# Hybrid diffusion block on one core: expert weights applied at the slots, and another order for layer 0's first rows

## The chip, the core and the metric

One core of a Trainium2 chip runs the whole kernel in one launch. Its engines are TensorE (PE, matmuls; PEld its weight loads), VectorE (DVE), ScalarE (ACT), GpSimd (POOL) and SyncE (SP, which here only issues DMAs); ACT and POOL also issue DMAs on queues of their own. The 16 DMA engines of the core move all data between HBM and the on-chip memories, SBUF and PSUM. The metric is the device time of one execution in microseconds, lower is better.

## What is computed

Two layers over 512 latent tokens and 256 context tokens of width 1024. Each layer is a mixer and then a mixture of experts; the last layer computes no context output. Cut to what matters here:

```python
for l in range(2):
    sh1, sc1, gt1, sh2, sc2, gt2 = split6(silu(c) @ w_ada[l] + b_ada[l])       # the same for the context, from c_ctx
    lam = exp(sum(lq1 * lk1)) - exp(sum(lq2 * lk2)) + lam_init
    xn = rms_norm(h, g_norm_mix[l]) * (1 + sc1) + sh1
    p = xn @ w_in[l]                       # then attention, gating MLP, neighbourhood attention
    h = h + gt1 * merge_branches(...)
    xn2 = rms_norm(h, g_norm_ffn[l]) * (1 + sc2) + sh2
    h = h + gt2 * hier_moe(xn2)            # top-1 group, top-2 experts, weights top_w
    ...
return rms_norm(h, g_final)
def hier_moe(x):                           # each token: two experts, expert e with weight top_w
    ys = (silu(xb @ w_gate[e]) * (xb @ w_up[e])) @ w_down[e]
    return segment_sum(ys[dest] * w_sorted[:, None], ...)
```

So a token's residual gets gt2 * (w0 * y0 + w1 * y1), y0 and y1 from its two experts.

## The kernel before, in words

All values are float32. A product of the mixer is made of three matmuls on a high and a low part of each factor (`wh`, `wl` of the weights, made by `wsplit`; `xh`, `xl` of the rows, made by `modulate`, or by `high` and `low`), so that each weight unit of 256 columns costs 24 matmuls of 128x256 per row tile of 128 tokens. There are six row tiles, four latent (0 to 3) and two of the context (4 and 5). SP issues all weight loads from one program order; where a buffer is still in use, the issue waits.

**Start of layer 0** (`mixer`, lines 460 to 481 and the constants from line 170). SP issues the small loads (`cvec`, `vecs`, `bada`, `gsub`, `lamv`, `rbias`), then six row tiles of `x`, the first `w_in` unit and the eight halves of `w_ada`. For each row tile `rownorm` squares the rows on ACT (line 220), makes the factor on DVE and POOL (221, 222; POOL's pow takes the root) and scales the rows in place on ACT (224). PE transposes the scaled rows, four row tiles for each k of eight (`turn`, 400). `ada` multiplies the conditioning vector with `w_ada` in 32 small matmuls for each half (445), DVE adds the halves (448, 451), PE transposes the sum (453) and DVE writes it to `mod` (454); `scales` makes the factors of the modulation (392, 394). `modulate` then applies scale and shift on ACT while reading PSUM (407) and splits on DVE (408, 409). All this is done for four k, then for the other four. Then the products of the first unit run over the six row tiles (230 to 232), the context's turns and modulations between them, each followed by a gelu on ACT (490).

**Expert stream** (`moe`). The router has sorted the tokens to 17 lanes of 128 slots (the two weights of each token are in `topw`). For each lane, POOL gathers the rows of `xs` by index (`gather`, line 1909), PE transposes them (1923), `gateup` and `down` multiply with the experts' weights, which SP streams in 1 MB pieces in lane order (1933), ACT and DVE copy the two halves of the result from PSUM (1972, 1973), and POOL scatters the lane's 128 rows to the table `yb`, one row for each token and choice (1974). Stages of neighbouring lanes overlap: the down product of a lane runs behind the gate and up products of the next. A loop at the end handles blocks over the fixed lanes; its length is read from memory (2020). Near the end of the stream SP loads the gate rows `grow` (gt2, broadcast to all partitions).

**Combine** (class `Combine`). For a row tile SP loads both rows of each token from `yb` (2053). `pre` multiplies the second by its weight on ACT (2058), `add` multiplies the first and adds on DVE (2064) and multiplies by the gate row (2066), `resid` adds to the residual on DVE or POOL (2069), then come the square on ACT (2073), the root (221, 222), and either `diag` (a diagonal of the factors, 2080, which PE uses as the moving matrix to transpose and scale at once, 502) or, at the very end, `final` (2087) and a store. Between the layers, `first_units` runs this with the first two units of layer 1's mixer. Its order is set by a planner, `Weave`: each step has a list of engine times, and the planner places steps on engines, with `way` as the choice between two engines (DVE or POOL, ACT or DVE).

## Time and profile before

| | us |
|---|---|
| median of the runs shown (3 runs, 2616.36 to 2624.96) | 2620.15 |
| the profiled execution's own time | 2619.65 |
| its span in the trace | 2617.5 |
| PE busy | 2307.9 |
| DVE busy | 1123.2 |
| ACT busy | 690.7 |
| POOL busy | 384.6 |

The span is the time from the first to the last event in the trace; the execution's own time has 2.15 us around it. In order of time the program is: mixer 0 to about 895 us, expert stream 0 to about 1400, the combine with the first units of layer 1 to 1467, the rest of mixer 1 to about 2075, expert stream 1 to about 2577, and the last combine. A row of a timeline gives the start, the duration, the engine (SPq is SP's queue), the line of the kernel, the operation, the result and its operands, the number of instructions merged in it, and in brackets the idle time before with what ended it. In a row of windows the engines stand in the order PE, PEld, DVE, ACT, POOL. A PE row's "x16" is one stretch of 16 matmuls. The clock column gives the granted clock of PE as a share of its full 2.4 GHz.

### The profile page before, as it was taken

How to read it: one execution, taken by the hardware profiler on the slowest of the kernel's cores; microseconds unless marked ns; L12 is line 12 of the kernel's file. 1: busy time of each engine (PE TensorE's matmuls, PEld its weight loads, DVE VectorE, ACT ScalarE, POOL GpSimd, SP SyncE). 2: the span in 40 equal slices, each digit the busy share in tenths (PEclk: the TensorE clock that was granted, in tenths of full speed). 3: DMA queues.
4: the chain of work that ended last, by engine and by line, in shares of the span. 5: the costliest groups of instructions: out<-in, count | busy, mean ns of one | idle time of the engine just before them, and what ended most of it. 6: DMA issues, size and time to landing. Idle time of an engine off the chain costs nothing. (4 is left out here: it accounts for less than half of the span.)

```text
span 2617.5 us, 35788 instructions
## 1 busy us (share of the span) xinstructions
PE 2307.9 (88%) x14117; PEld 1563.5 (60%) x14117; DVE 1123.2 (43%) x2122; ACT 690.7 (26%) x1345; POOL 384.6 (15%) x335
## 2 busy tenths in 40 slices
PE   5999999899999799898885999999999799887983
PEld 4888788788887633333323788887777633332321
DVE  3456667677754611111004646676454611110103
ACT  4235656612212100000003325655222200000001
POOL 0101210222211101000000302212332000000002
PEclk8999999999999899999998999999999899999997
DMA  6311121265435599999997411123653799999994
GB/s 242 124 67 37 57 73 50 101 219 183 162 113 229 207 402 424 424 424 423 422 424 284 161 65 52 39 85 109 233 201 138 307 391 420 420 419 416 416 413 189
DMA packets 116714, 625.98 MB, mean 239 GB/s; under 512 B 17440, under 2 KB 23328, under 8 KB 57536
## 3 DMA queue, kind: packets, MB, share of 16 engines
q1 hardware_dynamic: 93232, 576.61, 55.8%
q0 software_dynamic: 13088, 32.60, 3.5%
q10 hardware_dynamic: 10224, 14.46, 1.5%
q8 instruction: 113, 1.85, 0.3%
q14 instruction: 57, 0.47, 0.1%
HBM read 599.93 MB, written 38.34 MB: 244 GB/s over the span
## 5 line engine op out<-in xcount | busy, mean ns | idle before, releaser
L1933 PE MATMUL pd<-ew,mh 128*32 128x512 f32 (+2 forms) x1472 | 259.6, 595 | 16.3 <-DMA ew<-in_w_down 12.2
L230 PE MATMUL pg<-xh,wh 128*128 128x512 f32 (+1 forms) x576 | 205.7, 357 | 0.0
L232 PE MATMUL pg<-xh,wl 128*128 128x512 f32 (+1 forms) x576 | 205.4, 357 | 0.0
L709 PE MATMUL pj<-xh,wh 128*128 128x512 f32 (+1 forms) x544 | 195.9, 360 | 10.8 <-DVE rt L829 3.9
L231 PE MATMUL pg<-xl,wh 128*128 128x512 f32 (+1 forms) x576 | 205.3, 356 | 0.0
L711 PE MATMUL pj<-xh,wl 128*128 128x512 f32 (+1 forms) x544 | 189.4, 348 | 0.0
L710 PE MATMUL pj<-xl,wh 128*128 128x512 f32 (+1 forms) x544 | 189.3, 348 | 0.0
L1933 PEld LDWEIGHTS pd<-ew,mh 128*32 128x32 f32 (+2 forms) x1472 | 90.6, 122 | 159.3 <-issue 116.2
L1933 PE MATMUL pu<-ew,mx 128*32 128x512 f32 (+2 forms) x768 | 154.4, 609 | 29.4 <-DMA ew<-in_w_up 29.3
L364 DVE SCALAR_TENSOR_TENSOR jk<-wr,crow 128x1024 bf16<-128x1024 f32 x128 | 155.7, 1217 | 47.6 <-DMA wr<-in_w_adaT 45.2
L1933 PE MATMUL pg<-ew,mx 128*32 128x512 f32 (+2 forms) x768 | 152.7, 609 | 21.2 <-DMA ew<-in_w_gate 21.1
L1951 DVE TENSOR_TENSOR mh<-mh,pu 128x512 f32<-128x512 f32 x34 | 23.4, 688 | 331.0 <-PE pu L1933 331.0
L1974 POOL DMA_INDIRECT yb<-mt,si x34 | 37.1, 1093 | 850.2 <-DVE mt L1973 577.9
L213 POOL TENSOR_TENSOR wl<-wr,wh 128x1024 fp32r<-128x1024 f32 x48 | 119.6, 2491 | 282.2 <-ACT wh L212 282.2
L1933 PE MATMUL pg<-ew,mt 128*32 128x512 f32 (+2 forms) x704 | 140.3, 623 | 17.9 <-DMA ew<-in_w_gate 16.9
L1933 PE MATMUL pu<-ew,mt 128*32 128x512 f32 (+2 forms) x704 | 134.4, 596 | 20.9 <-DMA ew<-in_w_up 20.7
L1973 DVE COPY mt<-pd 128x512 f32<-128x512 f32 x34 | 23.5, 692 | 282.9 <-ACT mt L1972 274.3
L1950 ACT ACTIVATE mh<-pg 128x512 f32<-128x512 f32 x34 | 20.3, 597 | 459.0 <-PE pg L1933 459.0
L1322 ACT ACTIVATE sg<-pg 128x512 f32<-128x512 f32 x72 | 38.0, 528 | 369.7 <-PE pg L232 362.1
L938 PE MATMUL S<-K,Q 128*128 128x256 f32 (+3 forms) x544 | 111.8, 333 | 12.9 <-ACT E L976 6.2
L1960 DVE COPY mh<-trh 128x512 f32<-128x512 f32 x34 | 23.5, 691 | 226.0 <-PE trh L1957 226.0
L709 PEld LDWEIGHTS pj<-xh,wh 128*128 128x128 f32 x544 | 102.8, 189 | 29.5 <-DVE rt L829 5.5
(369 smaller groups left out, 4801.8 us busy)
## 6 DMA issues: line engine op xcount, KB each, us to landing
ew<-in_w_gate SPq DMA_DIRECT2D x128, 1024.0 KB
ew<-in_w_up SPq DMA_DIRECT2D x128, 1024.0 KB
ew<-in_w_down SPq DMA_DIRECT2D x128, 1024.0 KB
wr<-in_w_in SPq DMA_DIRECT2D x54, 1024.0 KB
wr<-in_w_adaT SPq DMA_DIRECT2D x80, 512.0 KB
br<-in_w_branch SPq DMA_DIRECT2D x24, 512.0 KB
adw<-in_w_ada SPq DMA_DIRECT2D x8, 1024.0 KB
wr<-in_w_out SPq DMA_DIRECT2D x8, 1024.0 KB
```

The costliest lines, as they stand in the source:

```text
L213: (eng or V).tensor_sub(lo, x, hi.bitcast(F32))
L230: PE.matmul(ps, lh, rh, start=(i == 0), stop=False)
L231: PE.matmul(ps, lh, rl, start=False, stop=False)
L232: PE.matmul(ps, ll, rh, start=False, stop=(i == n - 1))
L364: V.scalar_tensor_tensor(jk, ad["t"][:, i % 2 * D:(i % 2 + 1) * D], 1.0, ad["c"][:, s], op0=ALU.mult, op1=ALU.mult, accum_out=modT[al][:, ...
L709: PE.matmul(ps, lh, rh, start=(k == 0), stop=False)
L710: PE.matmul(ps, lh, rl, start=False, stop=False)
L711: PE.matmul(ps, ll, rh, start=False, stop=(k == KC - 1))
L938: PE.matmul(ps, q[:, m, part, c], K[:, m, ks], start=(part == 0), stop=(part == 1))
L1322: S.activation(sg[:, o:o + n], ps[:, :n], AF.Sigmoid)
L1933: PE.matmul(ps[o:o + r], lt[:, k0 + k, o:o + r], w[:, k, c], start=(k0 + k == 0), stop=(k0 + k == kk - 1), **pos)
L1974: G.indirect_dma_start(out=yb[l], out_offset=bass.IndirectOffsetOnAxis(ap=idx, axis=0), in_=y, in_offset=None, bounds_check=2 * TT - 1, oo ...
```

## The change

Four things change.

**Start of layer 0.** SP issues `x` 0 to 3 first, then the halves of `w_ada` 0 and 2, the first `w_in` unit, `w_ada` 1 and 3, `x` 4 and 5 and only then `lamv`, `gsub` and `rbias`; `vecs` and `bada` are issued by ACT. The exponential of lambda is POOL's pow, later (`lambdas`). The rows are not scaled: `scale_of` makes a diagonal of factors, and `turn` multiplies with it instead of a transpose. The sums of the modulation are apart from its products (`adasum`) and have a PSUM tile of their own; the split of the first unit lies between. The first two row tiles' products begin with the first four k (`share`) ahead of the last four modulations.

**Expert stream.** `topw` is transposed by PE, copied, and written by a POOL DMA to a table `tw` in DRAM, in the row order of `yb`. `weigh` gathers a lane's 128 weights from it by the scatter's indices into a column of `wsl`. The gate rows are loaded at the stream's start on ACT's queue; in layer 0 `gates` picks the latent or the context gate for each slot (the difference of the rows times a 0/1 mask, plus one of them). Two DVE steps multiply the down product by weight and gate as they read PSUM, instead of the two copies. The buffers of `y`, `hd` and `ht` are single instead of double.

**Combine.** `pre` and the multiply by the gate go, `add` is one addition, and `resid` is on DVE alone.

**Planner.** Costs change, and steps of the two ways that share a port are named "V+P" and "G+P".

```diff
     S.activation(cpad[:, :, 0:2], cvec, AF.Silu)
     vecs = const.tile([128, 4, KC], F32, name="vecs")
-    SP.dma_start(vecs, a["gvec"])
+    S.dma_start(vecs, a["gvec"])
     bada = const.tile([128, 2, 48], F32, name="bada")
-    SP.dma_start(bada, a["b_ada"])
+    S.dma_start(bada, a["b_ada"])
     gsub = const.tile([128, 2], F32, name="gsub")
...
+    def lambdas(pool):
+        lamv = pool.tile([128, 2, 4, 64], F32, name="lamv")
+        SP.dma_start(lamv, a["lam"].rearrange("(o l) f d -> o l f d", o=1).to_broadcast([128, 2, 4, 64]))
+        SP.dma_start(gsub, a["gsub"])
+        SP.dma_start(rbias, a["rbias"].rearrange("(o l) e -> o l e", o=1).to_broadcast([128, 2, 36]))
...
+        lx = ls.rearrange("p l i -> p (l i)")
+        V.memset(lamv[:, 0, 2, :4], math.e)
+        G.tensor_tensor(lx, lamv[:, 0, 2, :4], lx, op=ALU.pow)
...
+        def scale_of(nt):
+
+            r = rownorm(nm, xr[nt // 3][:, nt % 3, :], None)
+            dg0[nt] = nm.tile([128, 128], F32, name=f"dg{nt}")
+            V.tensor_scalar_mul(dg0[nt], ident, r)
...
-                PE.transpose(ps[:, i * 128:(i + 1) * 128], xr[nt // 3][:, nt % 3, k * 128:(k + 1) * 128], ident)
+                PE.matmul(ps[:, i * 128:(i + 1) * 128], xr[nt // 3][:, nt % 3, k * 128:(k + 1) * 128], dg0[nt],
+                          start=True, stop=True)
...
-            ps = pp.tile([128, 512], F32, tag="pj", name="adaps", bufs=2)
+            ps = part[n, half] = adb[half]
             for k in range(4):
                 for g in range(4):
                     PE.matmul(ps[32 * g:32 * g + 32, :128], cpad[:, 4 * half + k, :], w[:, k, g * 128:(g + 1) * 128],
                               start=(k == 0), stop=(k == 3), tile_position=(0, 32 * g))
+
+        def adasum(n, half):
+
+            ps = part.pop((n, half))
...
+            def xload(*tiles):
+                for nt in tiles:
+                    SP.dma_start(xr[nt // 3][:, nt % 3, :], a["x"][nt * 128:(nt + 1) * 128, :])
+
             raws = []
-            for n in (0, 2, 1, 3):
+
+            def aload(n):
                 for half in range(2):
                     t = nm.tile([128, KC, 256], F32, tag="ada", name="adw", bufs=8)
                     SP.dma_start(t, a["w_ada"][n, half])
                     raws.append((n, half, t))
-            for nt in range(6):
-                x = xr[nt // 3][:, nt % 3, :]
-                rownorm(nm, x, x)
-            wsplit(0)
+
+
+            xload(*range(4))
+            aload(0)
+            aload(2)
+            pump(1)
+            aload(1)
+            aload(3)
+            xload(4, 5)
+            lam = lambdas(nm)
+            next(lam)
+            for nt in range(4):
+                scale_of(nt)
...
+            def adas(four, split=None):
+
+                for i, x in enumerate(four):
+                    ada(*x)
+                    if i:
+                        adasum(*four[i - 1][:2])
+                    if split is not None and i in (1, 2):
+                        wsplit(0, 1)
+                adasum(*four[-1][:2])
+
+            adas(raws[:4])
+            scales(0, 4)
+            for k in range(4):
+                modulate(k, 0, ps[k])
+            ps = [turn(k, 0) for k in range(4, KC)]
+            adas(raws[4:], 0)
+            scales(4, KC)
+            early = {nt: pp.tile([128, 512], F32, tag="pj", name="pjx", bufs=2) for nt in range(2)}
+
+            def share(nt, k0, k1):
+                c = slice(nt * 128, nt * 128 + 128)
+                wh, wl = ready[0]
+                for k in range(k0, k1):
+                    PE.matmul(early[nt][:, :256], xk(xh, k, c), wh[:, k], start=(k == 0), stop=False)
+                    PE.matmul(early[nt][:, :256], xk(xh, k, c), wl[:, k], start=False, stop=False)
+                    PE.matmul(early[nt][:, :256], xk(xl, k, c), wh[:, k], start=False, stop=(k == KC - 1))
+
+            for nt in range(2):
+                share(nt, 0, 4)
+            for k in range(4, KC):
+                modulate(k, 0, ps[k - 4])
+            for nt in (4, 5):
+                scale_of(nt)
+            for nt in range(2):
+                share(nt, 4, KC)
+            cps = [turn(k, 1) for k in range(4)]
...
+                row_bc(grow["l"], rows(l, 3)[0], S)
...
+        def gates(n):
+
+            if last:
+                return grow["l"]
+            V.scalar_tensor_tensor(grow["s"], grow["d"], msl[:, n:n + 1], grow["l"], op0=ALU.mult, op1=ALU.add)
+            return grow["s"]
+
+        def weigh(n, idx):
+
+            G.indirect_dma_start(out=wsl[:, n:n + 1], out_offset=None, in_=tw[l],
+                                 in_offset=bass.IndirectOffsetOnAxis(ap=idx, axis=0),
+                                 bounds_check=2 * TT - 1, oob_is_err=False)
...
-            y = yo_[i % 2]
-            S.copy(y[:, :512], pd[:, :512])
-            V.tensor_copy(y[:, 512:], pd[:, 512:])
+            y = yo_[0]
+            for c in (slice(0, 512), slice(512, D)):
+                V.scalar_tensor_tensor(y[:, c], pd[:, c], wsl[:, n:n + 1], g[:, c], op0=ALU.mult, op1=ALU.mult)
...
+        trw = pp.tile([128, 512], F32, tag="tr", name="trw", bufs=2)
+        PE.transpose(trw[:2 * NT, :128], route.topw.rearrange("p k n -> p (k n)"), ident)
+        rws = ep.tile([12, 128], F32, name="rws")
+        V.tensor_copy(rws[:2 * NT], trw[:2 * NT, :128])
+        G.dma_start(tw[l].rearrange("(r p) o -> r (p o)", p=128), rws[:2 * NT])
+        for i in range(2):
+            weigh(plan[i], si[:, plan[i]:plan[i] + 1])
+        if not last:
+            V.tensor_copy(msl[:, :NS], gi)
+            V.tensor_scalar(msl[:, :NS], msl[:, :NS], TL - 0.5, None, op0=ALU.is_gt)
...
+                    weigh(n, si[:, n:n + 1])
+            if not i and not last:
+                row_bc(grow["d"], rows(l, 3)[1], S)
+                V.tensor_sub(grow["d"], grow["d"], grow["l"])
...
-        grow = raw_tile("ex").rearrange("p (k d) -> p k d", k=2)
-        for s in range((NT + 3) // 4):
-            row_bc(grow[:, s, :], rows(l, 3)[s])
...
-            def pre(self, nt):
+            def add(self, nt):
                 y = y2[nt]
-                self.done.add(nt)
-                S.activation(y[:, 1, :], y[:, 1, :], AF.Copy, scale=route.topw[:, 1, nt:nt + 1])
-
-            def add(self, nt):
-                if nt not in self.done:
-                    self.pre(nt)
-                y = y2[nt]
-                V.scalar_tensor_tensor(y[:, 0, :], y[:, 0, :], route.topw[:, 0, nt:nt + 1], y[:, 1, :],
-                                       op0=ALU.mult, op1=ALU.add)
-                V.tensor_mul(y[:, 0, :], y[:, 0, :], grow[:, nt // 4, :])
-
-            def resid(self, nt, way):
-                (V, G)[way].tensor_add(hrow(nt), hrow(nt), y2[nt][:, 0, :])
+                V.tensor_add(y[:, 0, :], y[:, 0, :], y[:, 1, :])
+
+            def resid(self, nt):
+                V.tensor_add(hrow(nt), hrow(nt), y2[nt][:, 0, :])
```

On SP, the start of the program: before, all small loads stand ahead of `x` (`x_159` and `x_160` are its two buffers of three row tiles, `adw` the halves of `w_ada`, `wr` a unit of `w_in`).

```order
3 L175 DMA vecs<-in_gvec 128x32
4 L177 DMA bada<-in_b_ada 128x96
5 L179 DMA gsub<-in_gsub 128x2
6 L181 DMA lamv<-in_lam 128x512
7 L183 DMA rbias<-in_rbias 128x72
8 L460 DMA x_159<-in_x 128x1024 x3
9 L460 DMA x_160<-in_x 128x1024 x3
10 L297 DMA wr<-in_w_in 128x2048
11 L466 DMA adw<-in_w_ada 128x2048 x8
```

The same place with the change (`x_142` and `x_143` are the buffers of `x`):

```order
2 L170 DMA cvec<-in_cond 128x16
3 L481 DMA x_142<-in_x 128x1024 x3
4 L481 DMA x_143<-in_x 128x1024
5 L488 DMA adw<-in_w_ada 128x2048 x4
6 L303 DMA wr<-in_w_in 128x2048
7 L488 DMA adw<-in_w_ada 128x2048 x4
8 L481 DMA x_143<-in_x 128x1024 x2
9 L188 DMA lamv<-in_lam 128x512
10 L189 DMA gsub<-in_gsub 128x2
11 L190 DMA rbias<-in_rbias 128x72
```

Four row tiles of `x` stand behind `cvec` alone now, the first unit of `w_in` in the middle of `w_ada`, and the last two row tiles and three small loads behind all of it.

On DVE, the last combine, before: a row tile has two steps ahead of its residual, three of the four residual adds are on POOL and don't stand here (`en` and `ew` hold the two rows of `yb`, `ex` the gate row or the final gain, `hr` the residual, `rn` the factors).

```order
1712 L2064 SCALAR_TENSOR_TENSOR ew<-ew,topw 128x1024
1713 L2066 TENSOR_TENSOR ew<-ew,ex 128x1024
1714 L2064 SCALAR_TENSOR_TENSOR ew<-ew,topw 128x1024
1715 L2066 TENSOR_TENSOR ew<-ew,ex 128x1024
1716 L2064 SCALAR_TENSOR_TENSOR ew<-ew,topw 128x1024
1717 L2066 TENSOR_TENSOR ew<-ew,ex 128x1024
1718 L221 TENSOR_SCALAR rn<-rn 128x1
1719 L2064 SCALAR_TENSOR_TENSOR en<-en,topw 128x1024
1720 L2066 TENSOR_TENSOR en<-en,ex 128x1024
1721 L221 TENSOR_SCALAR rn<-rn 128x1
1722 L2069 TENSOR_TENSOR hr<-hr,en 128x1024
```

The same place with the change:

```order
1755 L2162 TENSOR_TENSOR ew<-ew 128x1024
1756 L2165 TENSOR_TENSOR hr<-hr,ew 128x1024
1757 L2162 TENSOR_TENSOR ew<-ew 128x1024
1758 L227 TENSOR_SCALAR rn<-rn 128x1
1759 L2165 TENSOR_TENSOR hr<-hr,ew 128x1024
1760 L2162 TENSOR_TENSOR ew<-ew 128x1024
1761 L227 TENSOR_SCALAR rn<-rn 128x1
1762 L2165 TENSOR_TENSOR hr<-hr,ew 128x1024
1763 L2162 TENSOR_TENSOR en<-en 128x1024
1764 L227 TENSOR_SCALAR rn<-rn 128x1
1765 L2165 TENSOR_TENSOR hr<-hr,en 128x1024
```

DVE adds the two rows of a token and then adds them to the residual, tile by tile, with every residual add on DVE.

On POOL, a stretch of layer 1's expert stream, before: gathers of rows and scatters of results in turn.

```order
232 L1909 DMA mx<-xs_143,gi 128x1024
233 L1974 DMA yb_145<-mt,si 1024x1024
234 L1909 DMA mx<-xs_143,gi 128x1024
235 L1974 DMA yb_145<-mt,si 1024x1024
236 L1909 DMA mx<-xs_143,gi 128x1024
```

The same stretch with the change:

```order
263 L1982 DMA mx<-xs_126,gi 128x1024
264 L2047 DMA wsl<-tw_124,si 128x1
265 L2063 DMA yb_128<-mt,si 1024x1024
266 L1982 DMA mx<-xs_126,gi 128x1024
267 L2047 DMA wsl<-tw_124,si 128x1
268 L2063 DMA yb_128<-mt,si 1024x1024
269 L1982 DMA mx<-xs_126,gi 128x1024
```

Behind each gather of rows there is now a gather of weights for the same lane, ahead of the scatter of an earlier lane.

## Rows read from the trace of the kernel before

**Rows 1.** The page, PE's busy tenths in 40 equal slices of the span.
```profile
PE   5999999899999799898885999999999799887983
```

**Rows 2.** Windows: stretch, length, busy us (instructions) by engine, PE's clock, DMA share, GB/s.
```profile
8.00:41.50 33.50, 14.53 (x159) 11.71 (x160) 8.43 (x28) 18.11 (x25) 3.30 (x6) 0.84 1.02 425
...
100.00:700.00 600.00, 572.83 (x3836) 503.77 (x3835) 395.27 (x758) 259.91 (x569) 100.44 (x91) 1.00 0.31 104
950.00:1380.00 430.00, 382.20 (x1998) 136.88 (x1987) 53.14 (x112) 27.14 (x46) 30.28 (x28) 0.99 1.01 423
...
1420.00:1460.00 40.00, 33.27 (x228) 31.69 (x228) 31.77 (x51) 17.44 (x35) 11.42 (x9) 0.84 0.27 105
```

**Rows 3.** Timeline of SP's queue, start of the program.
```profile
3.54 3.77 SPq L460 DMA_DIRECT2D x<-in_x  x6
```

**Rows 4.** Timeline of ACT, 0 to 80 us.
```profile
9.92 1.06 ACT L220 ACTIVATE jk<-x 128x1024 f32<-128x1024 f32 x1 [1.24 <-DMA x<-in_x]
...
11.92 1.15 ACT L224 ACTIVATE x<-x,rn 128x1024 f32<-128x1024 f32 x1 [0.86 <-POOL rn L222]
...
38.02 2.79 ACT L407 ACTIVATE xn<-nt,mod,mA 128x512 f32<-128x512 f32 x4 [7.73 <-DVE mA L394]
49.43 2.79 ACT L407 ACTIVATE xn<-nt,mod,mA 128x512 f32<-128x512 f32 x4 [8.62 <-DVE mA L394]
...
55.25 0.39 ACT L490 ACTIVATE vv<-pjx 128x256 f32<-128x256 f32 x1 [1.74 <-PE pjx L232]
...
71.82 0.38 ACT L490 ACTIVATE vv<-pjx 128x256 f32<-128x256 f32 x1 [2.45 <-PE pjx L232]
74.64 0.38 ACT L490 ACTIVATE vv<-pjx 128x256 f32<-128x256 f32 x1 [2.44 <-PE pjx L232]
```

**Rows 5.** Timeline of PE, the last two halves of the modulation.
```profile
46.01 1.95 PE L445 MATMUL adaps<-adw,cpad 128*32 128x128 f32 x64
```

**Rows 6.** Timeline between the layers, all engines.
```profile
1411.84 1.28 DVE L2064 SCALAR_TENSOR_TENSOR ew<-ew,topw 128x1024 f32<-128x1024 f32 x1 [0.32 <-ACT ew L2058]
1413.16 1.23 DVE L2066 TENSOR_TENSOR ew<-ew,ex 128x1024 f32<-128x1024 f32 x1
1414.42 1.22 DVE L2069 TENSOR_TENSOR hr<-hr,ew 128x1024 f32<-128x1024 f32 x1
...
1418.85 0.29 DVE L2080 TENSOR_SCALAR ew<-ident,rn 128x128 f32<-128x128 f32 x1 [0.69 <-POOL rn L222]
...
1419.19 3.78 PE L502 MATMUL nt<-ew,hr 128*128 128x128 f32 x16 [20.30 <-DVE ew L2080]
...
1447.12 3.36 POOL L2069 TENSOR_TENSOR ex<-ex,en 128x1024 f32<-128x1024 f32 x1 [3.61 <-DVE en L2066]
...
1448.28 3.29 DVE L2066 TENSOR_TENSOR ew<-ew,ex 128x1024 f32<-128x1024 f32 x1
...
1454.44 0.58 PE L230 MATMUL pjx<-wh,xh 128*128 128x256 f32 x1 [2.74 <-DVE xh L524]
...
1467.12 0.40 PE L709 MATMUL pj<-xh,wh 128*128 128x512 f32 x1
```

**Rows 7.** Timeline of the last combine, all engines.
```profile
2587.03 1.15 ACT L2058 ACTIVATE ew<-ew,topw 128x1024 f32<-128x1024 f32 x1 [10.69 <-DMA ew<-yb]
...
2592.09 3.25 DVE L2066 TENSOR_TENSOR ew<-ew,ex 128x1024 f32<-128x1024 f32 x1
...
2609.46 1.28 DVE L2087 SCALAR_TENSOR_TENSOR en<-hr,rn,ex 128x1024 f32<-128x1024 f32 x1
```

**Rows 8.** DMA view of 0.5 to 4 us: packets by size, and the queue's share.
```profile
DMA packets 606, 0.14 MB, mean 39 GB/s; under 512 B 576, under 2 KB 576, under 8 KB 606
...
q1 hardware_dynamic: 606, 0.14, 17.6%
```

**Rows 9.** The page: the software queue (packets, MB, share), and POOL's scatters.
```profile
q0 software_dynamic: 13088, 32.60, 3.5%
...
L1974 POOL DMA_INDIRECT yb<-mt,si x34 | 37.1, 1093 | 850.2 <-DVE mt L1973 577.9
```

141 lines of the change are left out of this document (73 added, 68 removed).

## The prediction

> **What bounds the kernel now.** I read the page first for the shape: TensorE (PE) is busy for over 70% in nearly all slices, with the first, one in the middle and the last the lowest or near it [rows 1]. Then the windows by stage, which say what holds the full slices. In the first mixer PE works 572.83 of 600 us while the DMA engines are busy for 0.31: PE is the bound. In the expert stream the DMA engines are at 1.01 and PE works 382.20 of 430: the stream is the bound, at 423 GB/s [rows 2]. So what ends the lead-in of a mixer or a stream earlier moves all that follows, and what adds to a stream's transfers lengthens it. Three places are neither: the first 50 us, some 65 us between the layers, and the last 40 us. For these I read the timelines.
>
> Start. The DMA engines are busy from 8 to 41.5 us (1.02, 425 GB/s) [rows 2], yet PE's first product waits for a chain: ACT squares a row tile (1.06), waits 0.86 for the root and scales it (1.15), 3.07 us a round and six rounds, before it modulates the first four k at 38.02 and the last four at 49.43; the first product is done by 55.25 [rows 4]. x is issued only at 3.54 [rows 3].
>
> Between the layers. For one row tile DVE does 1.28 + 1.23 + 1.22 us behind ACT's copy, and PE starts at 1419.19 after 20.30 us without work. Later POOL takes one residual add (3.36 us), and DVE's multiply beside it takes 3.29 instead of 1.23; PE then waits 2.74 us for DVE's cast, and the first units end at 1467.12 [rows 6].
>
> End. The same stall: DVE's multiply takes 3.25 beside a residual add on POOL, and the last final step starts at 2609.46 [rows 7].
>
> **The change part by part.**
>
> *Start.* Removed: six scalings of 1.15 and the waits of 0.86 from ACT's chain; the small loads lamv, gsub, rbias, vecs and bada from ahead of x. Moved: x 4 and 5 behind all weights, their squares behind the modulations, the context's turns between products, the products of the first four k of two row tiles ahead of the last four modulations. Added: a 128x128 diagonal per tile on DVE (0.29, as the same step between the layers [rows 6]), hidden by the wait for weights. x is now second on SP, issued about 1.2 us in instead of 3.54, and I let its first bytes land near 2.2. From there I take the stream as saturated. Up to the last half of w_ada stand four x tiles of 512 KB, eight halves of 1 MB and one w_in unit of 1 MB, 11.5 MB; at 425 GB/s that is 27.1 us, so it ends at 29.3, and with 1.7 us from the last byte to the release at 31.0. Behind it PE has 32 small matmuls: the row has 1.95 us for 64 without a break [rows 5], so 1.0, or 1.8 if the clock is low; then the sums and the transpose, 1.5 as before (46.01 + 1.95 to 49.43). The last four modulations start at 34.3 instead of 49.43: **−15.1**. The squares (4 x 1.25 from about 5 us, a root and a diagonal) are done near 11, long before the weights, so they cost nothing; without the weights' wait they would be the chain again, near 12. Further on, the gelus of the six row tiles stood at 55.25 to 74.64, 19.4 us for five products of 2.82 (71.82 to 74.64) [rows 4], so 5.3 us of holes, in which the context's modulations lay. Half of the holes should close: **−2.4**. Together −17.5. The low end is 12: x keeps its 6.4 us between issue and first square (3.54 to 9.92), and the holes stay. The high end is 20, with all holes gone. What holds the start next is the stream of weights itself.
>
> The trace has 425 and 423 GB/s in two stages [rows 2]. The Trainium skill ("DMA: Bandwidth & Descriptors", Specifications) gives a limit of about 358 GB/s from HBM for one core; by that, an estimate, the 11.5 MB would take 32 us, and the time would come out 5 us higher, at 2590. The rows decide against it.
>
> *Between the layers.* Removed per row tile: ACT's copy (1.15) and DVE's multiply (1.23); the scalar_tensor_tensor (1.28) becomes an add (1.22, as the residual). Moved: all residual adds to DVE. The first tile's data is there near 1410.6 (1411.84 less ACT's copy). Then 1.22 + 1.22 + the square (1.25) + root, diagonal and one more tile's add between them (2.6) bring PE's first turn to 1416.9, **−2.3**. DVE has 6 x (3.73 − 2.44) = 7.7 us less to do; the 2.1 us that it lost beside POOL go, and the wait of 2.74 behind them. The floor is PE's own work: eight products of 2.82 and six turns of about 2, 35 us behind 1416.9, end at 1452 against 1467.12. I take **−15** in all, since PE then waits for nothing long; the ends are −8 (DVE's steps alone) and −17.
>
> *End.* The landings stay: the first at 2587.03, the others 2.5 us apart (1 MB at 424 GB/s). With 1.22 + 1.22 on DVE behind each, the last residual ends at 2597.1; the four finals (1.25 each) run from there to 2602.2, with the last square and root beside the first of them. Before, the last ended at 2610.74: **−8.5** (−7.5 to −9.5). The stores behind it stay.
>
> *Expert streams.* Added in each lane: a gather of 128 values of 4 bytes, issued by POOL; two DVE steps of about 0.7 us from PSUM (half of 1.28) where ACT and DVE copied; in layer 0 a DVE step of 1.28 for the gate. A scatter's issue takes POOL 1.09 us, and POOL sits 850 us idle before its 34 scatters [rows 9], so another issue finds room. DVE's steps lie beside PE's wait for weights; if that cover went, a lane would lose about 1.4 us. What is left is the stream. Packets: 606, of which 576 under 512 bytes, took 17.6% of 16 engines over 3.5 us [rows 8], 16 ns each, so 128 take 0.13 us of the stream, and 34 gathers 4.4. Upper end: the software queue's mean packet, 3.5% of 16 x 2617.5 us over 13088, is 0.112 us [rows 9], so 0.9 us a gather, 30 us. Lower end: nothing, if they fit into pauses. I take 4.4, since the rows of small packets are the nearer. The gate's rows (512 KB, 1.24 us: two in layer 0, one in layer 1) come from the stream's end, where PE's last lanes hid them, to its beginning: 3.7 at most, 0 at least; I take 1.9. Together **+6.3**, 0 to 12 by these two. The weight table's transpose and copy at a stream's start lie where PE waits for the gathers of rows: nothing; if a gather of the weights comes late, DVE holds that lane's scatter, two lanes after the issue.
>
> Sum: −17.5 − 15 − 8.5 + 6.3 = −34.7. Against the profiled execution's 2619.65 (0.5 below the median of the runs shown) that is **2585**. Its ends: 2573 (20 + 17 + 9.5, nothing added) and 2604 (12 + 8 + 7.5, 12 added).
>
> **The rivals.**
>
> *A: start and boundary hardly move.* The weights' stream and DVE's casts were the bound there already, and PE, with less to do, stays at a low granted clock; the window between the layers has 0.84 [rows 2], and at the lower of the two levels (1.2 GHz against 2.4) a product takes twice 2.82. Against it: shorter waits leave PE fewer holes. With half of the low ends (6 and 4), the end's 8.5 and +6.3 it gives 2607.
>
> *B: the 4-byte gathers cost like full packets,* 30 us instead of 4.4: 2611, so 0.3% below the time of before, about what a measurement of this kernel can just tell from no change. For it: the same software queue. Against it: [rows 8]. The Trainium skill (same page and section) puts the smallest transfer at line rate at 512 bytes, with a read-modify-write below; the 16 ns are of such packets, and no run here shows them as writes of 4 bytes.
>
> *C, slower: the gathers hold the stream.* Place: the lanes; POOL's queue holds the next gather of rows behind a scatter that waits for DVE, which waits for the weights. The other parts win 41 us, less 1.9; so from 1.15 us a gather (0.144 us a packet on its engine) the streams lose more than all else wins. At 0.2 us a packet it is 1.6 x 34 = 54 us, and 2635. For it: nothing in the trace shows a 4-byte indirect gather. Against it: the mean of far larger packets is 0.112 [rows 9], and two lanes lie between issue and use.
>
> *D: the start does not follow the weights,* for one because w_in's unit or its split is late: only its low end or less (0 to 5) arrives; 2597 to 2602, inside the range.
>
> **How the numbers follow.** The forecast 0.72, D 0.10, A 0.08, B 0.06, C 0.04. The range 2571 to 2605 holds the forecast's ends and D, and leaves out A, B, C and the forecast's tails, just under 2 in 10 with them. Faster by over 0.3% (7.9 us): the forecast, D, A and a third of B, so 0.91; the same: most of B, with a little of C, 0.05; slower 0.04.
>
> **What would show it.** Right: modulations of the first four k near 22, of the last four near 34, the first product done near 40, the DMA engines full from 3 us on; between the layers no DVE step of 128x1024 over 1.4 us, and the first units over in some 50 us from the last expert instead of 68; the last final step starting 14 us after the first landing instead of 22; each stream about 3 us longer. Wrong: DVE's steps from PSUM waiting for the gathered weights, a stream longer by over 10 us, ACT still the chain of the start, or PE still waiting for DVE's casts between the layers.

## The result, and the profile after

The changed kernel takes 2590.76 us (median of 4 runs, 2588.95 to 2592.67), the kernel before in the same comparison 2618.96 us (4 runs, 2616.36 to 2624.96). The ratio is 0.9893, with a 95% interval of 0.9878 to 0.9907: 28 us faster. The forecast was 2585 us with a range of 2571 to 2605. The profiled execution took 2588.95 us, with a span of 2587.1; before it was 2619.65 and 2617.5. One execution of a kernel below, the one without gathers, fell into a slower state (2891.59 us at a granted clock of 0.74, where the others have 0.97) and is left out.

The page gives the same shape as [rows 1], with a fuller first slice:

```profile
PE   7999999899999698888886999999999789887984
```

To see where 30.4 us of span went, I cut both traces at the same events: the sixth gelu on ACT, the router's reciprocal in each layer, the end of the last fixed lane's down product, the first product of the unit that follows the first two in mixer 1, and the last final step on DVE.

| stage, us | before | change | difference |
|---|---|---|---|
| start, to the sixth gelu | 74.6 | 60.3 | −14.3 |
| rest of mixer 0, to the router's reciprocal | 840.2 | 840.5 | +0.3 |
| expert stream 0, to the end of its last fixed down product | 484.1 | 492.1 | +8.0 |
| between the layers, to the next unit's first product | 68.2 | 53.8 | −14.4 |
| rest of mixer 1, to the router's reciprocal | 624.7 | 626.2 | +1.5 |
| expert stream 1 | 483.9 | 483.6 | −0.3 |
| last combine, to the start of the last final step | 33.8 | 25.3 | −8.5 |
| from there to the end of the span | 8.1 | 5.3 | −2.8 |

The windows by stage, columns as in [rows 2], with the stream's window moved by the 14 us that it starts earlier:

```profile
8.00:41.50 33.50, 26.15 (x358) 22.32 (x357) 15.26 (x41) 11.20 (x17) 1.29 (x3) 0.95 0.96 388
100.00:700.00 600.00, 570.67 (x3822) 501.17 (x3821) 398.43 (x765) 259.11 (x567) 108.59 (x93) 1.00 0.29 103
936.00:1366.00 430.00, 379.76 (x1958) 136.99 (x1954) 82.89 (x143) 17.73 (x30) 43.56 (x41) 0.99 1.01 419
1400.00:1440.00 40.00, 28.78 (x230) 28.38 (x231) 33.99 (x62) 19.30 (x39) 6.62 (x6) 0.83 0.60 237
```

PE works 26.15 us between 8 and 41.5 us, where it worked 14.53. The stream has the same DMA share, 1.01, at 419 GB/s where it had 423. That fall is the first thing that the prediction has no step for.

The start on ACT, against [rows 4]: no scaling between the squares, the last four modulations at 36.73 instead of 49.43, the sixth gelu at 60.34 instead of 74.64.

```profile
4.87 1.06 ACT L226 ACTIVATE jk<-x 128x1024 f32<-128x1024 f32 x1 [0.85 <-DMA x<-in_x]
...
23.18 2.78 ACT L422 ACTIVATE xn<-nt,mod,mA 128x512 f32<-128x512 f32 x4 [13.05 <-DVE mA L400]
...
36.73 2.79 ACT L422 ACTIVATE xn<-nt,mod,mA 128x512 f32<-128x512 f32 x4 [8.89 <-DVE mA L400]
...
43.09 0.38 ACT L554 ACTIVATE vv<-pjx 128x256 f32<-128x256 f32 x1
...
60.34 0.38 ACT L554 ACTIVATE vv<-pjx 128x256 f32<-128x256 f32 x1 [2.44 <-PE pjx L238]
```

PE in the same time (L414 the turns, L460 the modulation's matmuls): no row waits for a weight's DMA. The second turns start when ACT has read a PSUM buffer and take 5.47 us, the matmuls of the sums come right behind them, and each later step waits for DVE's sums. The margin is small: by the semaphores in the trace the last half of `w_ada` has landed whole at 32.78, and PE comes to its matmuls at 33.85.

```profile
11.32 4.63 PE L414 MATMUL nt<-dg,x 128*128 128x128 f32 x26 [0.63 <-DVE dg L408]
15.88 1.95 PE L460 MATMUL adp<-adw,cpad 128*32 128x128 f32 x64
...
24.01 5.47 PE L414 MATMUL nt<-dg,x 128*128 128x128 f32 x32 [1.53 <-ACT xn L422]
29.41 1.95 PE L460 MATMUL adp<-adw,cpad 128*32 128x128 f32 x64
...
33.85 1.08 PE L460 MATMUL adp<-adw,cpad 128*32 128x128 f32 x32 [0.26 <-DVE mod L473]
```

Between the layers, DVE's and PE's timelines, against [rows 6]: two steps of 1.22 for a row tile and none of 3.29; PE's first turn comes 17.8 us behind the last down product's end (1392.9) instead of 20.3, and the next unit begins 36.0 us later.

```profile
1404.89 1.22 DVE L2162 TENSOR_TENSOR ew<-ew 128x1024 f32<-128x1024 f32 x1
1406.14 1.22 DVE L2165 TENSOR_TENSOR hr<-hr,ew 128x1024 f32<-128x1024 f32 x1
```

```profile
1410.69 5.35 PE L566 MATMUL nt<-ew,hr 128*128 128x128 f32 x32 [17.75 <-DVE ew L2176]
...
1446.70 0.39 PE L778 MATMUL pj<-xh,wh 128*128 128x512 f32 x1
```

The windows from the first turn to the next unit's first product, before and then after, show where the rest of the gain lies. The same matmuls (289 and 288 records) keep PE busy for 41.20 us before and 35.48 after, at a granted clock of 0.85 and 0.96; PE's idle time falls from 6.7 to 0.5 us. So of the 11.9 us that this stretch is shorter, 5.7 are matmuls that run faster and 6.2 are closed waits.

```profile
1419.19:1467.12 47.93, 41.20 (x289) 39.62 (x289) 37.88 (x63) 22.66 (x47) 11.42 (x9) 0.85 0.26 97
```

```profile
1410.69:1446.70 36.01, 35.48 (x288) 35.08 (x289) 29.17 (x61) 19.28 (x44) 5.13 (x5) 0.96 0.40 153
```

The change has one more part, which its list above leaves out: the length of the loop of blocks is read before the last lanes and not behind them. Little can come from it here: the combine's first loads are issued 6.2 us behind the last down product instead of 6.8, and its first step starts 12.0 us behind it, where it was 11.8.

The last combine on DVE, against [rows 7]: from the first landing at 2568.05 to the last final step 13.8 us, where it was 22.4.

```profile
2568.05 1.23 DVE L2162 TENSOR_TENSOR ew<-ew 128x1024 f32<-128x1024 f32 x1 [10.07 <-DMA ew<-yb]
...
2575.68 1.23 DVE L2162 TENSOR_TENSOR en<-en 128x1024 f32<-128x1024 f32 x1
...
2576.94 1.22 DVE L2165 TENSOR_TENSOR hr<-hr,en 128x1024 f32<-128x1024 f32 x1
...
2581.84 1.28 DVE L2183 SCALAR_TENSOR_TENSOR en<-hr,rn,ex 128x1024 f32<-128x1024 f32 x1
```

Behind the last final step, POOL's closing instructions (the view of the program's last line on POOL, before and then after; duration min/median/max in ns). The longest DRAIN takes 9.49 us before and 4.10 after. It starts 2.26 us ahead of the last final step in both, so before it ends 7.2 us behind that step's start, 2.9 us later than SP has seen the last store land (4.3), and after it ends at 1.8, ahead of the stores.

```profile
L2225 POOLq DRAIN  x3: 51/109/9493, 2607.2 to 2617.2; - x3
```

```profile
L2320 POOLq DRAIN  x3: 46/109/4102, 2579.6 to 2586.8; - x3
```

In the lanes, the page's rows against [rows 9]: 1152 packets more on the software queue for 0.1% more of its time, POOL idle for 821 us ahead of the scatters, and the two new DVE steps (0.747 us) waiting for PE's product, not for the weights. The page of the kernel without gathers (below) has 13152 packets on this queue, so 34 gathers make 1088, 32 each and not the 128 of the prediction: in the trace a gather is 16 packets of 32 bytes, 15 ns each, and 16 of 4 bytes, 9 ns each.

```profile
q0 software_dynamic: 14240, 32.63, 3.6%
...
L2063 POOL DMA_INDIRECT yb<-mt,si x34 | 37.5, 1103 | 821.4 <-DVE mt L2062 561.0
...
L2062 DVE SCALAR_TENSOR_TENSOR mt<-pd,wsl,mh 128x512 f32<-128x512 f32 x68 | 47.9, 747 | 243.7 <-PE pd L2007 236.6
```

### The profile page after: what moved, and what is told of

It is laid out like the page before. It is cut to its first block, busy times and chain, and to the rows that moved or that the text cites. A ratio compares the mean times of both kernels' runs of the same rounds, so it can differ in the third digit from the quotient of the medians.

```text
span 2587.1 us, 35911 instructions
## 1 busy us (share of the span) xinstructions
PE 2307.5 (89%) x14167; PEld 1561.3 (60%) x14167; DVE 1152.6 (45%) x2186; ACT 650.4 (25%) x1292; POOL 402.3 (16%) x363
## 5 line engine op out<-in xcount | busy, mean ns | idle before, releaser
L2026 ACT ACTIVATE mh<-pg 128x512 f32<-128x512 f32 x34 | 20.3, 597 | 690.4 <-PE pg L2007 690.4
L2062 DVE SCALAR_TENSOR_TENSOR mt<-pd,wsl,mh 128x512 f32<-128x512 f32 x68 | 47.9, 747 | 243.7 <-PE pd L2007 236.6
```

The source lines that it names most:

```text
L2062: V.scalar_tensor_tensor(y[:, c], pd[:, c], wsl[:, n:n + 1], g[:, c], op0=ALU.mult, op1=ALU.mult)
```

## The experiments

Three questions were open: what lengthens stream 0 by 8 us and stream 1 by nothing; what holds the start at 36.7 us where I had 34.3; and whether the gain of the combine is POOL's or DVE's. All stages are cut as in the table above. The kernel before took 2617.8 to 2619.0 us in each of the five comparisons, so kernels of different comparisons can be set side by side to about 1 us.

| kernel | median us (lowest to highest) | start: last modulations | reciprocal 0 | stream 0 | between | mixer 1 | stream 1 | combine | tail |
|---|---|---|---|---|---|---|---|---|---|
| before | 2618.96 (2616.36 to 2624.96) | 49.43 | 914.8 | 484.1 | 68.2 | 624.7 | 483.9 | 33.8 | 8.1 |
| before again | 2618.95 (2615.87 to 2621.74) | | 915.4 | 485.0 | 69.4 | 625.7 | 481.2 | 33.7 | 8.1 |
| before, buffers shifted | 2618.60 (2617.79 to 2623.25) | | 913.3 | 489.6 | 68.6 | 621.2 | 484.3 | 33.9 | 8.1 |
| before, residual on DVE | 2614.03 (2608.74 to 2617.68) | | 911.3 | 484.3 | 66.2 | 624.8 | 481.8 | 31.1 | 8.2 |
| change | 2590.76 (2588.95 to 2592.67) | 36.73 | 900.8 | 492.1 | 53.8 | 626.2 | 483.6 | 25.3 | 5.3 |
| no gathers | 2591.85 (2589.94 to 2593.26) | 39.29 | 904.4 | 489.0 | 54.2 | 629.0 | 481.5 | 25.2 | 8.2 |
| gathers twice | 2594.55 (2593.59 to 2596.28) | 36.54 | 900.9 | 490.6 | 54.3 | 627.8 | 488.5 | 24.9 | 5.4 |
| no gate rows | 2590.10 (2588.16 to 2594.24) | 36.01 | 899.5 | 489.4 | 54.0 | 628.8 | 485.8 | 25.3 | 5.3 |
| buffers aligned | 2583.88 (2580.76 to 2587.44) | 37.44 | 902.1 | 488.3 | 54.3 | 621.9 | 484.9 | 25.0 | 5.3 |
| turns later | 2593.53 (2591.72 to 2597.14) | 38.74 | 903.8 | 491.7 | 53.8 | 626.1 | 484.2 | 25.2 | 5.3 |
| residual on POOL | 2597.30 (2596.68 to 2599.50) | 35.87 | 900.4 | 491.9 | 54.1 | 628.7 | 483.9 | 31.4 | 5.3 |
| old start | 2605.68 (2602.72 to 2608.88) | 49.53 | 915.2 | 491.4 | 54.2 | 631.2 | 484.5 | 25.3 | 5.3 |
| w_in later | 2593.10 (2591.49 to 2594.28) | 39.11 | 900.8 | 492.2 | 53.9 | 628.7 | 483.7 | 25.0 | 5.3 |
| aligned, PE kept busy | 2585.15 (2582.66 to 2586.90) | 35.57 | 898.7 | 487.9 | 54.2 | 626.3 | 483.1 | 25.3 | 5.3 |

Kernels with the change's streams repeat stream 0 within 491.4 to 492.2 us and stream 1 within 483.6 to 484.5; the kernels with before's streams lie at 484.1 to 485.0 and 481.2 to 483.9. Mixer 1 moves by some 5 us from profile to profile at the same count of matmuls, so a single profile says nothing about it.

### No gathers, gathers twice, no gate rows, and before again

```diff
-        V.memset(wsl, 0.0)
+        V.memset(wsl, 1.0)
...
         def weigh(n, idx):
-            G.indirect_dma_start(out=wsl[:, n:n + 1], ...)
+            return
```

> This kernel leaves out the 34 gathers of weights; all slots get the weight 1.0, so the output has no expert weights in it. Measured from the router's reciprocal to the last down product of a fixed lane, the change lengthened layer 0's stream by 8.1 us (476.3 to 484.4) and layer 1's by nothing. Theory G (the gathers' packets take it): layer 0's stream falls back by 5 us or more and its rate returns from 419 to 424 GB/s; whole kernel 5 to 6 us faster than the change. Theory R (the rate of layer 0's stream is set by something else that the change moved, and the gathers are nearly free): the rate stays at 419 and the stream falls by 2 us at most, 2 by my price of 16 ns a packet. Full-packet price (rival B of the prediction): 30 us faster than the change, which the change's trace already speaks against.

```diff
+        wsd = const.tile([C, NS + 1], F32, name="wsd")
...
-            G.indirect_dma_start(out=wsl[:, n:n + 1], ...)
+            for c in (wsd[:, n:n + 1], wsl[:, n:n + 1]):
+                G.indirect_dma_start(out=c, ...)
```

> This kernel issues every gather of weights twice, the first into a column that nobody reads. Theory G: layer 0's stream 5 us longer again, the rate 414 GB/s. Theory R: 0 to 2 us longer in each layer, whole kernel 0 to 4.4 us slower than the change. Rival C (POOL's queue or DVE's wait for the weights decides from some number of issues on): DVE's steps from PSUM start to wait for wsl, and the streams grow by tens of us; POOL's issue of 1.0 us beside its idle time of 821 us before the scatters speaks against it.

```diff
-                row_bc(grow["l"], rows(l, 3)[0], S)
+                V.memset(grow["l"], 1.0)
...
-                row_bc(grow["d"], rows(l, 3)[1], S)
+                V.memset(grow["d"], 1.0)
```

> This kernel fills the gate rows of layer 0 and layer 1 with ones instead of loading them at the start of the streams; the output has no gates of the experts in it. My term: 1.9 us of 3.7 for three loads of 512 KB. Theory R and G both expect up to 2.5 us from layer 0's stream and up to 1.2 from layer 1's, whole kernel 2 to 4 us faster than the change. If the rate of layer 0 goes back to 424 GB/s here, the loads on a second queue slow the stream, and the stream falls by 8.

> The kernel before, once more, for its trace. If the rate of layer 0's stream (423 to 424 GB/s) and the 4.4 us between the last DMA packet and the end of the span are properties of the kernel, both come again within 1 GB/s and 0.5 us; if they vary from execution to execution, the 8 us that the change loses in layer 0's stream and the 2.8 us that it wins at the very end are partly that variation.

Without the gathers the streams are 3.1 and 2.1 us shorter (the expectation counts to the start of the last down product, 7.8 us earlier, with the same difference); doubled, stream 1 is 4.9 longer, and stream 0 is 2.3 longer than the kernel below that shares its rate. That is 5 to 7 us for 34 gathers, 0.15 to 0.21 us each, against my 0.13, and nowhere near the 0.9 of a full packet; each value is from one profile, and the smaller ones are hardly above what stream 1 varies by. The packets' own time does not explain it: 15 and 9 ns on each engine are 0.8 us for 34 gathers. Why a gather takes the stream more than that stays open. Neither theory came out whole: G missed the rate, R the size. The gate rows cost stream 0 2.7 us, as much as the two loads' 2.5; stream 1 did not gain without its row (485.8), and the kernel as a whole hardly did (2590.10 against 2590.76). So neither explains the rate: without gathers and without rows stream 0 still runs at 420 and 419 GB/s, and with twice the gathers it runs at 423. The window from 936 to 1366 us of the kernel without gathers, then of the one with twice:

```profile
936.00:1366.00 430.00, 380.08 (x1982) 138.34 (x1978) 82.99 (x143) 17.77 (x30) 30.29 (x28) 1.00 1.01 420
```

```profile
936.00:1366.00 430.00, 380.24 (x1987) 137.66 (x1990) 83.02 (x143) 17.77 (x30) 56.85 (x54) 0.99 1.01 423
```

In the latter DVE's steps still wait for PE and not for the weights (the view of the tile wsl, who it waited for), which leaves rival C nothing. The one wait for a scatter fits the single buffer of `y`; the change has it too, in the last fixed lane of layer 0:

```profile
  PE pd L2009: 234.4, 33
  issue: 11.3, 34
  DMA yb<-mt,si: 7.1, 1
```

The kernel before again ran its stream 0 at 424 GB/s and had the tail of 8.1 us, so both belong to the program. The kernel without gathers was no faster as a whole (2591.85 against 2590.76): its profile has a start that is 3.6 us longer, within what the start varies by, and a tail that is 3 us longer. The tail is the gathers' doing: POOL's closing DRAIN takes 9.65 us without them, as long as in the four kernels on before's text (9.49), 6.88 with twice the gathers, and 4.10 in all others. So the gathers lengthen the streams and shorten the end; why the DRAIN depends on them stays open.

### Where the buffers lie

What the doubled gathers had changed besides the gathers was an extra column tile in the constants: it moved all weight buffers behind it. In the placement of the compiled programs, all of layer 0's 16 buffers start 32 bytes past a multiple of 64 in the change, and at a multiple of 64 before and in the kernel with twice the gathers. Of the other kernels, those without gathers, without gate rows and with the old start have the change's placement and 419 to 420 GB/s, and before with the residual on DVE has before's and 424. Two kernels test the offset alone.

```diff
     ls = const.tile([128, 2, 2], F32, name="ls")
+    const.tile([128, 8], F32, name="pad")
...
+        if last:
+            wp.tile([128, 8], F32, tag="pad", name="pad", bufs=1)
         return hs, route, weights, st, es_
```

> The change with 32 bytes of padding in the constants and in layer 1's weight pool, so that all 16 weight buffers of both expert streams start at a multiple of 64 bytes in a partition (in the change all start 32 bytes off; before, layer 0's were at multiples of 64, and 9 of layer 1's 16). Theory A (the offset of the buffers sets the rate): layer 0's stream goes from 419 to 424 GB/s and is some 4 us shorter, layer 1's gains as much; whole kernel 4 to 8 us faster than the change. Theory G2 (gathers or rows lower the rate): nothing changes, 419 and 417 GB/s, within 1 us in each stream.

The kernel before got the first of these paddings only.

> The kernel before with 32 bytes of padding in the constants alone, so that layer 0's weight buffers, and the 9 of layer 1 that were at multiples of 64, start 32 bytes off. Theory A: layer 0's stream falls from 424 to 419 GB/s and grows by 4 to 5 us, layer 1's falls by 0 to 2 GB/s; whole kernel 4 to 6 us slower than before. Theory G2: no difference from before.

The windows of stream 0, with the change aligned (936 to 1366 us) and with before shifted (950 to 1380 us):

```profile
936.00:1366.00 430.00, 380.27 (x1986) 137.25 (x1978) 82.95 (x143) 18.06 (x31) 43.55 (x41) 0.99 1.01 423
```

```profile
950.00:1380.00 430.00, 379.12 (x1974) 136.40 (x1970) 52.55 (x111) 27.14 (x46) 30.25 (x28) 0.99 1.01 419
```

Both rates follow the offset: 423 for 419 in the change, 419 for 423 before, and stream 0 is 3.8 us shorter and 4.6 to 5.5 us longer. A padding moves every buffer behind it by 32 bytes; that it acts through the weights' buffers is inferred from their share of the bytes. Layer 1 does not follow: 417 GB/s aligned as not aligned, 418 before with 9 of 16 buffers aligned; what holds it there stays open. As a whole the aligned change is the fastest kernel, 2583.88 us, ratio 0.9869 (0.9854 to 0.9884) to before; the second kernel with this padding (below) has 2585.15. That is 5.6 to 6.9 us faster than the change, as theory A had it, but only some 4 of them are in stream 0. The shifted kernel before was not measurably slower (ratio 1.0003, 0.9994 to 1.0012): in its profile a mixer 1 of 621.2 us gives back what the stream loses. Why that mixer is shorter there is not settled; the aligned change has 621.9 and its sibling 626.3.

### The start: turns later, w_in later, PE kept busy, old start

```diff
-            ps = [turn(k, 0) for k in range(4, KC)]
-            adas(raws[4:], 0)
+            ps = []
+            adas(raws[4:], 0, lambda: ps.extend(turn(k, 0) for k in range(4, KC)))
...
                 for i, x in enumerate(four):
+                    if i == 2 and then is not None:
+                        then()
                     ada(*x)
```

> The change with the turns of the last four k placed on PE behind the first two halves of the second group of modulation weights instead of ahead of all four. Theory P (at the start PE's order and its low clock hold the last four modulations, which began at 36.7 us, not the weights' stream): the turns leave the chain and the modulations begin 1 to 2.5 us earlier, the first product is done as much earlier, and the kernel is 1 to 3 us faster. Theory W (my prediction: the weights' stream holds them): no change at the start, within 0.5 us.

```profile
25.34 1.93 PE L460 MATMUL adp<-adw,cpad 128*32 128x128 f32 x32 [1.70 <-DMA adw<-in_w_ada]
27.75 1.94 PE L460 MATMUL adp<-adw,cpad 128*32 128x128 f32 x32 [0.48 <-DMA adw<-in_w_ada]
29.62 4.25 PE L414 MATMUL nt<-dg,x 128*128 128x128 f32 x32
...
35.87 1.08 PE L460 MATMUL adp<-adw,cpad 128*32 128x128 f32 x32 [0.26 <-DVE mod L473]
```

PE's timeline shows the weights now: two halves land at 25.3 and 27.7, 2.4 us apart, and by the semaphores the last has landed at 32.7, not at my 31.0. But PE waits for the first two, its matmuls of 32 take 1.93 instead of 1.08 at a granted clock of 0.50, and the turns behind end at 33.9; the modulations began 2 us later, not earlier. Neither theory came out: this order let the stream and the low clock add up.

```diff
+            aload(1)
+            aload(3)
             pump(1)
-            aload(1)
-            aload(3)
```

> The change with the first w_in unit loaded behind all eight halves of w_ada, so that the last four halves land 2.5 us earlier. Theory W (the weights' stream holds the last four modulations): they begin 2 to 2.5 us earlier than in the change's runs, whose values were 35.9 to 37.4 us. Theory P (the turns and the chain of sums on PE and DVE hold them): no change beyond what the turns' own time makes (3.8 us at a granted clock of 1.00, 5.5 to 6.5 at 0.5 to 0.8), and the first products may come later, since their weights land last.

```profile
25.20 6.36 PE L414 MATMUL nt<-dg,x 128*128 128x128 f32 x32 [1.53 <-ACT xn L422]
31.49 1.96 PE L460 MATMUL adp<-adw,cpad 128*32 128x128 f32 x64
```

The last half has landed at 30.6 instead of 32.8 and nothing comes of it: the turns take 6.36 us at a granted clock of 0.50 from 24 to 30 us and end behind that landing, and the modulations begin at 39.11. Over the profiles the turns' time and the modulations go together: 3.84 us with 35.9 and 36.0, 5.47 with 36.5 to 37.4, 6.4 to 6.5 with 39.1 and 39.3. At the short end the stream is close behind: in the kernel with the residual on POOL, with turns of 3.84, PE came to the last half at 33.01 and the half had landed at 32.88. Weights earlier and a full clock together were not tried. In the change the granted clock was 1.00 from 16 to 24 us, while PE worked 4.65 of 8 us, and 0.61 from 24 to 27. The next kernel keeps PE at work.

```diff
+                    PE.matmul(adp[:, 384:], ident, ident, start=True, stop=True)
...
+            fill(12)
             ps = [turn(k, 0) for k in range(4)]
...
+            fill(4)
             ps = [turn(k, 0) for k in range(4, KC)]
```

> The change with all weight buffers at multiples of 64 bytes (as in the earlier run with padding, 2583.9 us) and with 16 matmuls of the identity whose result nobody reads, 12 ahead of the first turns and 4 ahead of the second, where PE waits. Theory C (at the start PE at the lower granted clock holds the modulations): the two groups of turns take 3.8 us or less instead of 4.6 to 5.9 and 3.8 to 6.5, the first modulations begin at 22 to 23 us, the last at 34.5 to 36, and the kernel is 1 to 2 us faster than with the padding alone. If the extra matmuls do not raise the clock, they only delay the turns: the modulations begin as late as before or 1 us later.

```profile
23.21 1.16 PE L510 MATMUL adp<-ident 128*128 128x128 f32 x8 [0.26 <-DVE mod L474]
24.49 3.84 PE L415 MATMUL nt<-dg,x 128*128 128x128 f32 x32
```

With four idle matmuls ahead of them the second turns run at the full clock, 3.84 us, and the modulations begin at 35.57, 1.9 us sooner than in the aligned kernel. That the idle matmuls did it is not shown: of the seven other kernels with this order of the start, two (no gate rows, residual on POOL) had the full clock and turns of 3.84 without them. The twelve ahead of the first turns did not help: those took 4.80 us at a granted clock of 0.59. The whole time, 2585.15 against 2583.88, does not show 2 us either way; the start's part is seen in the trace alone (reciprocal at 898.7 instead of 902.1).

> The change with the start of the kernel before: small loads first, rows scaled on ACT, sums inside each half of the modulation, products behind all modulations. If the start's gain passes through whole (mixer 0 behind it is bound by PE and took 843.0 and 843.3 us in the two kernels), the time is 14 us above the change (my prediction had 17.5), the router's reciprocal moves back from 901 to 915 us, and the rest stays. Rival (part of the gain is lost later, in a stream or at the clock): under 10 us.

The old start in the change gives 2605.68 us, 14.9 above the change, with the reciprocal 14.4 later and the sixth gelu at 74.75. So what the start gains passes whole through mixer 0. (The expectation's 843 us count from the fifth gelu; from the sixth they are 840.2 and 840.5.)

### Who adds the residual

```diff
-                V.tensor_add(hrow(nt), hrow(nt), y2[nt][:, 0, :])
+                (G if nt in ((4, 5), (0, 1, 2))[l] else V).tensor_add(hrow(nt), hrow(nt), y2[nt][:, 0, :])
```

> The change with five of the ten residual adds on POOL again, those that were there before (row tiles 4 and 5 between the layers, 0 to 2 at the end). Theory S (the shared port: DVE's steps with two operands in SBUF stand still while POOL adds): DVE's adds beside them take 3.2 to 3.3 us instead of 1.22, the end grows by 4 to 6 us of its 8.5 and the time between the layers by 2 to 4 us; whole kernel 6 to 10 us slower than the change. Theory L (the gain came from less work on DVE alone): only POOL's longer adds show, 2 us at the end and nothing between the layers.

DVE and then POOL in the last combine:

```profile
2572.93 2.16 DVE L2162 TENSOR_TENSOR ew<-ew 128x1024 f32<-128x1024 f32 x1 [1.34 <-DMA ew<-yb]
...
2585.36 0.15 DVE L227 TENSOR_SCALAR rn<-rn 128x1 f32<-128x1 f32 x1 [3.93 <-ACT ew L2169]
```

```profile
2571.68 2.33 POOL L2165 TENSOR_TENSOR hr<-hr,ew 128x1024 f32<-128x1024 f32 x1 [10.11 <-DMA ew<-yb]
2575.46 0.57 POOL L228 TENSOR_TENSOR rn<-rn,mhalf 128x1 f32<-128x1 f32 x1 [1.45 <-DVE rn L227]
2576.02 2.90 POOL L2165 TENSOR_TENSOR hr<-hr,ew 128x1024 f32<-128x1024 f32 x1
```

The kernel loses 6.5 us, 6.1 of them in the last combine and 0.3 between the layers. The size is theory S's, the mechanism neither's. One DVE add beside POOL grew to 2.16, so the port is seen, but it is not the price: POOL's adds of 2.3 to 2.9 and its roots stand in one queue, and DVE, with little to do, waits for squares (3.93). Between the layers POOL's two adds come (1424 to 1429 us) when DVE has no step of 128x1024 left beside them, and cost nothing that stands out.

```diff
-                (V, G)[way].tensor_add(hrow(nt), hrow(nt), y2[nt][:, 0, :])
+                V.tensor_add(hrow(nt), hrow(nt), y2[nt][:, 0, :])
```

> The kernel before with all residual adds on DVE and nothing else (the planner's choice of POOL is ignored). Theory S (the port): no DVE step with two operands in SBUF takes over 1.4 us any more, the last final step comes 5 to 6 us sooner behind the first landing, the first units end 3 to 5 us sooner; whole kernel 8 to 11 us faster than before. Theory L (less work on DVE): the end gains 2 to 3 us since POOL's adds of 3.3 us become DVE's of 1.2, between the layers DVE has more to do, and nothing is gained there.

```profile
2581.07 1.28 DVE L2064 SCALAR_TENSOR_TENSOR ew<-ew,topw 128x1024 f32<-128x1024 f32 x1 [11.25 <-DMA ew<-yb]
...
2593.33 1.22 DVE L2069 TENSOR_TENSOR hr<-hr,ew 128x1024 f32<-128x1024 f32 x1
...
2599.54 1.28 DVE L2087 SCALAR_TENSOR_TENSOR en<-hr,rn,ex 128x1024 f32<-128x1024 f32 x1
```

This one gained 3.9 us (ratio 0.9985, 0.9976 to 0.9995): 2.7 in the last combine and 2.0 between the layers (3.2 against the second profile of before), the 2 to 3 of theory L at the end and less than theory S there. No DVE step is stretched any more, but with three steps per tile, 3.73 us together, DVE itself is the chain. So the two parts need each other: moving the adds is worth 2.7 us with three DVE steps per tile and 6.1 with two. The rest of the 14.4 us between the layers, 11 to 12, belongs to the steps that went into the lanes together with the planner's new costs; these two were not tried apart.

## Why the prediction was right

The time came out 5.8 us above the forecast, inside its range, and on the predicted side. The sum of the parts is nearer than some of them: a start that gained 3.2 us less than forecast and streams that lost 1.4 us more stand against 2.8 us at the very end that I had not predicted. Step by step:

- **Between the layers, −15: held.** Measured −14.4. The first turn came 2.5 us sooner (predicted 2.3), and from there to the next unit PE needs 36.0 us (predicted 35, as its own work), of which it works 35.5. So PE's own work is the floor there, as predicted. That floor is reached only because PE's busy time fell by 5.7 us with a higher granted clock; the sum has this unsaid, in that it takes every product at 2.82. Of the reasons given, the fights at the port are worth 2 to 3 us; the removed steps have the rest, not told apart from the planner's costs.
- **End, −8.5: held**, −8.5 to the last final step and 13.8 us behind the first landing (predicted 14). A further 2.8 us lie behind the last final step, where I had put nothing ("The stores behind it stay"). The stores did stay, 4.3 us to the last one's landing before and after; what went is POOL's closing DRAIN beyond them, which the gathers of the streams shorten. That is luck.
- **Start, −17.5: mis-sized, −14.3.** The step that failed is the time at which the last four modulations start, 34.3 us, which the sum lets follow the stream of weights alone. They began at 36.73 in the change, 35.6 to 39.3 over the runs. Part of the miss is the sum itself: 11.5 loads of 1024 KB are 12.06 million bytes, 28.4 us at 425 GB/s and not 27.1. The last half landed at 32.78, 1.8 us later than counted. (No row stands behind the 1.7 us from the last byte to the release; in the change's trace the 16 engines report that half between 31.15 and 32.78.) The other part is PE's own chain: turns at a low granted clock, then 32 matmuls and a sum at a time with DVE between them, so that PE comes to the half 1.1 us behind its landing. From there to the modulations it took 2.9 us where I had 3.3. Loading the weights earlier gained nothing while the turns were slow. The holes behind gave 1.6 us instead of 2.4 (17.25 us from the first gelu to the sixth, against 19.39, and 0.5 more to the first).
- **Expert streams, +6.3: right in size by luck, +7.7.** The gathers cost 5 to 7 us where I had 4.4, the rows 2.7 where I had 1.9. The 4.4 are near by chance: they were 128 packets of 16 ns a gather, and the page counts 32. Some 4 us of layer 0 are the buffers' offset of 32 bytes, for which I had no term; the parts add to more than stream 0 lost, and stream 1 lost nothing that a single profile shows (the mean of five profiles with the change's streams is 1.7 us above that of three with before's, which lie 2.7 apart). What the single buffers of `y`, `hd` and `ht` cost was not tried.
- **The 358 GB/s** of the Trainium skill ("DMA: Bandwidth & Descriptors", Specifications), by which the start would have been slower, is passed by the rows of the start and of both streams: 388 to 425 GB/s.
- **Rivals.** A had the low clock right for the start, but not its size, and wrong between the layers, where PE's granted clock was 0.96 instead of 0.85 from the first turn on, with fewer waits between. B's packet price and C's wait were both refuted by the doubled gathers, D by the old start.

## What to carry to other kernels

A weight or a gate that scales rows is cheapest where another engine waits anyway; here it left two serial stretches for streams that wait for DMA, and the stretches gained 22.9 us where the streams lost 7.7, part of that by the buffers' offset. Before a step is credited to one engine's removal, run it alone in both kernels: what POOL's adds cost depended on how full DVE was. After any change of small tiles look at the large buffers' start addresses, and compare the rate of a saturated stream to the last GB/s.

## What the hardware did that I had not expected

- Transfers into buffers that start 32 bytes past a multiple of 64 bytes run 1% slower (419 instead of 423 to 424 GB/s in layer 0's stream, both ways). The Trainium skill ("DMA: Bandwidth & Descriptors", How a descriptor splits into AXI transactions) speaks of 256-byte boundaries; here 9 of layer 0's 16 buffers start 192 bytes past one in the kernel before, 7 on one, and it has 424. Layer 1's stream stays at 417 to 418 with either placement.
- PE's granted clock at the start differs between profiles of kernels with the same start: 0.50 to 1.00 from 24 to 27 us. The lower of the two levels (1.2 GHz) lasts through most of the second turns in some and does not come in others, which goes with a start that moves by 3 us.
- A gather of 128 values of 4 bytes took the stream 0.15 to 0.21 us, though its 32 packets take each engine only 24 ns.
- POOL's closing DRAIN took 9.49 us in kernels with 34 gathers of rows and 34 scatters, 9.65 with these and the weight table's writes, 4.10 with 34 gathers of weights besides and 6.88 with 68. Where it is the longer, the end of the program waits for it and not for the last store.
